# Scoring new tokens four at a time, other slots for their value pages, and adding x at the end in a one-core decoder step

## The chip, the cores and the metric

The kernel runs on one core of a Trainium2 chip. The metric is the device time of one execution in microseconds; the median of the runs is compared. In the text, PE is TensorE (PEld its weight loads), DVE is VectorE, ACT is ScalarE, POOL is GpSimd and SP is SyncE, which issues all DMAs here.

## The reference, cut to what matters

One decoder layer is computed for a prompt of 1024 tokens and for 8 sequences of 4 new tokens each, all in fp32. RMSNorm(x) goes through one input projection. Four heads run a gated linear recurrence (HGRN2), eight heads run forgetting attention (FoX). The gated outputs are concatenated, multiplied by w_out and added to x, and a last RMSNorm follows:

```python
xp = xp + mixer_output(hg_o, hgate, fox_o, fgate, hg_norm_w[l], w_out[l], xp.dtype)
y_prompt = rmsnorm(xp, final_norm_w)
# new tokens: 256 past rows from two cache pages of 128, and the new rows
s = jnp.einsum('bqhd,bkhd->bhqk', q, k) * (D ** -0.5)
s = s + (cq[..., None] - c[:, :, None, :])
p = jax.nn.softmax(where(causal, s, -inf), axis=-1)
o = jnp.einsum('bhqk,bkhd->bqhd', p, v)
```

## The kernel before

The instruction order is written out by hand. Two programs are interleaved on every engine. The **foreground** is the FoX attention of the prompt: 32 steps, one for each head and quarter of the queries (`order`). A step transposes probabilities (T, line 965), weighs the values with them (W, tile `po`), computes scores of later steps (S, tile `ps`), takes exponentials of them (E, line 945 and the division on POOL, line 950) and gates the result (G). The **stream** (`projections`) is all other work: input projections, the new tokens' attention, the output projection.

`PLANS` writes a foreground step as a list of such letters and numbers. A number is a call of `fill`, which pulls pieces from the stream until the sum of their yields, called credits here, reaches the number times a factor. The factors are 7.6, 6.4, 4.4 and 3.0 for the four query quarters, so a step with quarter 0 to 3 draws 7.6, 6.4, 4.4 or 3.0 credits. In the last head pair (steps 24 to 31; quarters 0, 1, 0, 1, 2, 3, 2, 3) they are multiplied by `F3`. A credit is a weight written in the code and no time of the chip. When the foreground has ended, the rest of the stream runs alone.

In the last head pair the stream has this order:

- The end of the last gate projection. Then `wo_open` frees the memory of the normed input, and the remaining output weights are loaded.
- `out_half(tb, c)` for c = 0, 1 and tb = 0 to 3: the first four of eight k blocks of the output projection of prompt block tb, column half c. Each has 12 matmuls of 512 columns and 2.6 credits. x is loaded into a half tile by `x_load`, DVE adds the PSUM result to it (line 1296), and `out_spill` writes it to DRAM scratch `y_s`. With c = 0 it also issues `k_load`, `wo_load`, and at tb = 3 `decode_queries`, which clears a tile on POOL and fills it with eight small ACT copies (line 1132).
- `fox_decode`, the new tokens' attention, in two groups g of four sequences. A group's scores (`Sx[g]`) take for each sequence four key matmuls of 256 columns and four of 32 columns on the new keys (`kd`), 32 query columns wide, so each sequence owns 32 of the 128 PSUM partitions. An fp32 matmul shows as two matmuls in the trace. One sequence is finished before the next begins; it counts 1.9 credits. `soft(g)` is the softmax. The values are two matmuls of 512 columns for each sequence, 0.85 credits each, and one with the new values for each group (`vdf`). Group 0 of the scores stands ahead of `out_half(3, 1)`, group 1 and the values stand behind it.
- `out_proj(0)`, the new tokens' block `out_proj(NB)`, then `out_proj(1)` to `out_proj(7)`. For blocks 0 to 3 the first half is read back from `y_s` into a y tile (`out_load`), k blocks 4 to 7 are accumulated, and DVE adds them (line 1363). Blocks 4 to 7 are done whole.

Key pages use slots 100, 101, 102 and 5, twice. Value pages use slots 28, 4, 0 and 2, twice: the second four are loaded while the first four are used. A load that reuses a slot waits on SP for the readers of the slot, and all later DMAs wait behind it.

Of the kernel before, what the change touches and what calls it, by code (L numbers as in the profile page):

```python
# [70 lines left out]
def tile_hymba(ctx, tc, x_prompt, x_sample, x_b, x_d, cache_k_t, cache_v, cache_logf_t, state_hgrn, page_table,  # L71
# [1035 lines left out]
            SP.dma_start(lr[j * FH:(j + 1) * FH, PAST:], ld_s[j * DT:(j + 1) * DT].rearrange("t h -> h t"))  # L1107

    KT = (100, 101, 102, 5, 100, 101, 102, 5)

    def k_load(j):
        if j < DB:
# [2 lines left out]
                SP.dma_start(kT[:, b], cache_k_t[pages[2 * j + b]].rearrange("o p s -> (o p) s"))  # L1115

    def v_load(j):
        vp = U((28, 4, 0, 2)[j % 4], 1024, a=2)
        for b in range(2):
            SP.dma_start(vp[:, b], cache_v[0, pages[2 * j + b]].rearrange("a s h d -> s (a h d)"))  # L1120

# [14 lines left out]
    def fox_decode():  # L1136
# [35 lines left out]
            V.tensor_copy(PT[g], p[:, :256].rearrange("p (a t) -> p a t", a=2))  # L1172

        for g in range(2):
            if g:
                for j in range(4):
                    v_load(j)
                m_load(4, 0)
                m_load(5, 0)
            Sx.append(ps_pj()[:, :NK])  # L1180
            for j4 in range(4):
                j = 4 * g + j4
                kT = U(KT[j], 1024).rearrange("p (b a s) -> p a b s", b=2, a=4)
                for pr in range(4):
                    q = qb[:, pr, j].rearrange("p h t -> p (h t)")
                    mm(Sx[g][32 * j4:32 * j4 + 32, :PAST], q, kT[:, pr], pr == 0, pr == 3)
                    if pr == 1:
                        yield 0.9
                for pr in range(4):
                    q = qb[:, pr, j].rearrange("p h t -> p (h t)")  # L1190
                    mm(Sx[g][32 * j4:32 * j4 + 32, PAST:], q, kd[:, pr], pr == 0, pr == 3)
                k_load(j + 4)
                yield 1.0
            soft(g)
            yield 0.36
            if g == 0:
                yield None
        SP.dma_start(fw, bcast_row(final_norm_w, D))
        for g in range(2):
            po = ps_pj()  # L1200
            for j4 in range(4):
                j = 4 * g + j4
                vp = U((28, 4, 0, 2)[j4], 1024, a=2)
                for b in range(2):
                    mm(po[32 * j4:32 * j4 + 32], PT[g][:, b, 32 * j4:32 * j4 + 32], vp[:, b], b == 0, False)
                    i = 2 * j4 + b
                    if g == 0 and b:
                        v_load(j + 4)
                    if g and i % 2 == 0 and i < 6:
                        m_split(4 + i // 2, 0)  # L1210
                        if i == 0:
                            m_load(6, 0)
                    yield 0.85
            mm(po, PN[g], vdf, False, True)
            yield 0.85
            od = xd_f[0]
            A.activation(od, po, AF.Copy)
            defer(3, turn_out, g, od)
# [49 lines left out]
    def x_part(tb):  # L1268
        return U(tb // 2 * 2, D, a=2)[:, tb % 2]

    def x_load(tb, c):
        SP.dma_start(x_part(tb), xp[tb * 128:(tb + 1) * 128, 512 * c:512 * c + 512])

    def out_half(tb, c):

# [4 lines left out]
        for k in range(4):  # L1280
            if tb == c == 0:
                if k == 0:
                    m_split(2, 0)
                    m_split(3, 0)
                    wo_split(3, 0)
                if k in (1, 3):
                    for i in (k - 1, k):
                        x_load(i, 0)
            h, l = merged[k, 0]
            mm(ps, h[:, t], woh(k, cs), k == 0, False)  # L1290
            mm(ps, l[:, t], woh(k, cs), False, k == 3)
            mm(ps, h[:, t], wol(k, cs), False, False)
            if k < 3:
                yield 0.65
        yield 0.65
        V.tensor_add(y, y, ps)
        if c == 0:
            if tb < 3:
                wo_split(tb, 1)
            if tb == 2:  # L1300
                wo_split(3, 1)
            for j in ((0,), (1, 3), (2,), ())[tb]:
                k_load(j)
            if tb > 1:
                wo_load(4 + tb)
            if tb == 3:
                decode_queries()
        else:
            for k in (2 * tb, 2 * tb + 1):
                wo_split(4 + k % 4, k // 4)  # L1310
        if c == 0:
            defer(6, x_load, tb, 1)
            defer(4, out_spill, tb, c, y)
        else:
            out_spill(tb, c, y)

    def out_spill(tb, c, y):
        SP.dma_start(y_s[tb][:, 512 * c:512 * c + 512], y)
# [13 lines left out]
    def out_proj(tb, cuts=(0, 512, 1024)):  # L1332
# [4 lines left out]
        for i in range(len(cuts) - 1):  # L1337
            cs = slice(cuts[i], cuts[i + 1])
            ps = ps_pj()[:, :cuts[i + 1] - cuts[i]]
            if tb < NB:  # L1340
                t = slice((tb % 4) * 128, (tb % 4) * 128 + 128)
                k0 = 4 if tb < 4 else 0
                for k in range(k0, KB):
                    h, l = merged[k, tb // 4]
                    mm(ps, h[:, t], woh(k, cs), k == k0, False)
# [51 lines left out]
    def projections():  # L1397
# [26 lines left out]
        for c in range(2):  # L1424
            for tb in range(4):
                yield from out_half(tb, c)
                if c and tb == 2:
                    for us in dec:
                        if us is None:
                            break  # L1430
                        yield us
        yield from dec
        out_load(0)
        m_load(0, 1)
        m_load(1, 1)
        yield from wait_flag("half0")
# [16 lines left out]
            yield from out_proj(tb)  # L1453
        yield from out_proj(7, (0, 512, 768, 1024))

    F3 = 1.8
    stream.append(projections())
    log_forget()
    need("hq0")
# [23 lines left out]
    for n, (pr, i, q) in enumerate(order):  # L1483
# [15 lines left out]
        if pr == 3:  # L1499
            if s == 4:  # L1500
                flags.add("A")
                out_load(NB)
                out_load(1)
    gate_pop(True)
    flags.add("half1")
    while step() is not None:
# [50 lines left out]
```

## Time and profile before

| | us |
|---|---|
| runs (three) | 773.49, 773.97, 775.08 |
| median | 773.97 |
| the profiled execution, its own time | 775.96 |
| its span, first to last instruction | 774.2 |
| PE, PEld, DVE, ACT, POOL busy | 741.8, 665.5, 464.8, 363.5, 315.1 |
| mean granted TensorE clock | 0.985 |

Busy times are sums of the profile. Matmuls are pipelined, so their durations overlap; what a piece of PE work takes is read from start to start.

### The profile page before, as it was taken

How to read it: one execution, taken by the hardware profiler on the slowest of the kernel's cores; microseconds unless marked ns; L12 is line 12 of the kernel's file. 1: busy time of each engine (PE TensorE's matmuls, PEld its weight loads, DVE VectorE, ACT ScalarE, POOL GpSimd, SP SyncE). 2: the span in 40 equal slices, each digit the busy share in tenths (PEclk: the TensorE clock that was granted, in tenths of full speed). 3: DMA queues.
4: the chain of work that ended last, by engine and by line, in shares of the span. 5: the costliest groups of instructions: out<-in, count | busy, mean ns of one | idle time of the engine just before them, and what ended most of it. 6: DMA issues, size and time to landing. Idle time of an engine off the chain costs nothing.

```text
span 774.2 us, 13013 instructions
## 1 busy us (share of the span) xinstructions
PE 741.8 (96%) x4835; PEld 665.5 (86%) x4835; DVE 464.8 (60%) x973; ACT 363.5 (47%) x853; POOL 315.1 (41%) x332
## 2 busy tenths in 40 slices
PE   8999989999999999998999899989999899999996
PEld 7778989998999999998998899979988776577886
DVE  5775554747647565366447844785478776667422
ACT  5663555434242431136546654757466521555322
POOL 0442544364371753726434552536344533232101
PEclk9999999999999999999999999999999999999999
DMA  8211000101221113013001021101111596713521
GB/s 337 93 36 40 1 11 20 60 4 58 82 83 58 55 33 110 28 37 134 28 29 57 29 71 40 57 30 55 55 57 57 188 329 221 260 58 123 199 81 55
DMA packets 27569, 64.99 MB, mean 84 GB/s; under 512 B 5394, under 2 KB 6546, under 8 KB 27506
## 3 DMA queue, kind: packets, MB, share of 16 engines
q1 hardware_dynamic: 27506, 64.16, 24.3%
q8 instruction: 38, 0.62, 0.3%
q14 instruction: 25, 0.20, 0.1%
HBM read 47.27 MB, written 16.88 MB: 83 GB/s over the span
## 4 chain that ended last, share of the span: by engine, by line
PE 73%; DVE 13%; ACT 8%; issue 3%; DMA 2%; POOL 1%; SPq 1%; DVEq 0%; ACTq 0%; POOLq 0%
PE pj L95 53%; PE ps L95 11%; PE po L95 3%; PE pt L965 2%; DVE u L970 2%; DVE u L896 1%; PE pt L95 1%; DVE st L935 1%; ACT u L969 1%; ACT u L945 1%; DMA u<-in_x_prompt_dram 1%; DMA u<-in_w_dram 1%; ACT xhi L269 1%; DVE u L831 1%; DVE u L638 1%
## 5 line engine op out<-in xcount | busy, mean ns | idle before, releaser
L95 PE MATMUL pj<-xhi,u 128*128 128x352 f32 x1152 | 307.2, 331 | 0.9 <-DVE u L487 0.5
L95 PEld LDWEIGHTS pj<-xhi,u 128*128 128x128 f32 x1152 | 206.5, 190 | 3.1 <-DVE u L487 0.8
L95 PE MATMUL pj<-xlo,u 128*128 128x352 f32 x576 | 187.3, 325 | 0.0
L95 PE MATMUL ps<-u,u 128*128 128x64 f32 (+6 forms) x984 | 129.2, 272 | 3.5 <-ACT u L945 2.6
L95 PEld LDWEIGHTS ps<-u,u 128*128 128x128 f32 (+2 forms) x984 | 112.2, 178 | 12.9 <-ACT u L945 4.4
L950 POOL TENSOR_SCALAR u<-u,st 128x128 f32<-128x128 f32 (+3 forms) x64 | 48.7, 762 | 153.4 <-DVE st L948 87.7
L95 PEld LDWEIGHTS pj<-xlo,u 128*128 128x128 f32 x576 | 109.6, 190 | 0.7
L95 PE MATMUL pj<-u,xhi 128*128 128x260 f32 (+1 forms) x384 | 91.7, 332 | 5.7 <-DVE u L526 3.4
L945 ACT ACTIVATE u<-ps,st 128x512 f32<-128x512 f32 (+2 forms) x96 | 55.0, 578 | 50.3 <-DVE st L938 21.4
L95 PEld LDWEIGHTS pj<-u,xhi 128*128 128x128 f32 x384 | 65.2, 195 | 13.9 <-DVE u L526 3.0
L95 PE MATMUL pj<-h,u 128*128 128x512 f32 (+2 forms) x237 | 74.1, 384 | 0.8 <-DVE h L1086 0.8
L699 POOL TENSOR_TENSOR u<-u,u 128x256 f32<-128x256 f32 (+1 forms) x56 | 42.0, 751 | 76.5 <-PE ps L95 76.4
L970 DVE TENSOR_TENSOR u<-pt,u 128x512 fp32r<-128x512 f32 (+1 forms) x80 | 48.5, 632 | 28.4 <-ACT u L969 27.9
L95 PE MATMUL pj<-u,xlo 128*128 128x260 f32 (+1 forms) x192 | 63.8, 333 | 0.0
L969 ACT ACTIVATE u<-pt 128x512 fp32r<-128x512 f32 (+1 forms) x80 | 41.8, 552 | 41.1 <-PE pt L965 33.5
L935 DVE TENSOR_REDUCE st<-ps 128x1 f32<-128x512 f32 (+2 forms) x96 | 53.4, 556 | 12.2 <-PE ps L95 9.6
L95 PE MATMUL po<-u,u 128*128 128x256 f32 (+1 forms) x320 | 52.2, 287 | 8.5 <-DVE u L970 4.5
L95 PEld LDWEIGHTS po<-u,u 128*128 128x128 f32 x320 | 44.3, 189 | 15.4 <-DVE u L970 7.5
L95 PEld LDWEIGHTS pj<-h,u 128*128 128x128 f32 (+1 forms) x237 | 42.4, 186 | 10.3 <-issue 1.5
L95 PE MATMUL pj<-u,u 128*128 128x512 f32 (+3 forms) x174 | 46.1, 434 | 2.4 <-ACT u L1253 1.0
L95 PE MATMUL pj<-w,u 128*128 128x512 f32 (+2 forms) x125 | 47.4, 380 | 0.0
L700 POOL TENSOR_TENSOR u<-u,u 128x256 f32<-128x256 f32 (+1 forms) x56 | 43.6, 778 | 0.0
(252 smaller groups left out, 1147.0 us busy)
## 6 DMA issues: line engine op xcount, KB each, us to landing
u<-in_w_s_dram SPq DMA_DIRECT2D x24, 512.0 KB
out_dram<-u SPq DMA_DIRECT2D x12, 512.0 KB
u<-in_x_b_dram SPq DMA_DIRECT2D x8, 512.0 KB
u<-in_cache_k_t_dram SPq DMA_DIRECT2D x16, 256.0 KB
u<-in_cache_v_dram SPq DMA_DIRECT2D x16, 256.0 KB
m_s<-u SPq DMA_DIRECT2D x7, 512.0 KB
u<-m_s SPq DMA_DIRECT2D x14, 256.0 KB
w<-in_w_out_dram SPq DMA_DIRECT2D x12, 256.0 KB
```

Of the source, the lines that this page charges most:

```text
L95: PE.matmul(out, lhsT, rhs, start=start, stop=stop, skip_group_check=True)
L269: A.activation(xhi[:, k, t0:t0 + n], xt[:, k], AF.Copy)
L638: V.tensor_mul(f, f3[:, :, 0], f3[:, :, 1])
L699: G.tensor_mul(k4[:, :, 0, :], k4[:, :, 0, :], f3[:, eb, 1:2].to_broadcast([128, n, m]))
L700: G.tensor_mul(q4[:, :, 1, :], q4[:, :, 1, :], f3[:, eb, 0:1].to_broadcast([128, n, m]))
L831: V.tensor_copy(hi, vo[:, :, 64 * i:64 * i + 64])
L935: V.tensor_reduce(st[:, m:m + 1], ps, axis=AX.X, op=OP.min)
L945: A.activation(P[:, s], ps, AF.Exp, scale=-1.0, bias=st[:, lo:lo + 1], accum_out=st[:, 2 + m:3 + m])
L950: G.tensor_scalar(P[:, :e], P[:, :e], st[:, 4:5], 1.0, op0=OP.mult, op1=OP.mult)
L965: PE.transpose(p[:, c:c + 128], probs[n, b][:, j * 128:(j + 1) * 128], ident)
L969: A.activation(ph[:, :w], p[:, :w], AF.Copy)
L970: V.tensor_sub(pl[:, :w], p[:, :w], f32(ph[:, :w]))
```

## The change

- **Scores.** The four sequences of a group now take turns: for each of the four head pairs, one key matmul of every sequence, then the small ones in the same way. A group counts 2.46 credits in place of 7.96.
- **Order.** Group 0 of the scores now runs after `out_half(0, 1)`, group 1 after `out_half(2, 1)`; the values still run after `out_half(3, 1)`.
- **Values.** The pages of sequences 0 to 3 go into the key slots 100, 101, 102, 5 as soon as group 1 has read its keys, those of 4 to 7 into 28, 4, 0, 2 ahead of the values. Keys 0, 1 are loaded after `out_half(0, 0)`, keys 2, 3 after `out_half(1, 0)`. The final norm weights (slot 5) are loaded after the values.
- **x.** `out_half` no longer loads x; ACT copies the PSUM result and the spill is issued at once. x is loaded as one row tile for each block and POOL adds it to the read-back half in `out_proj(0)` to `out_proj(3)`.
- **F3** goes from 1.8 to 1.58.

```diff
+    VT = (100, 101, 102, 5, 28, 4, 0, 2)
     def v_load(j):
-        vp = U((28, 4, 0, 2)[j % 4], 1024, a=2)
+        vp = U(VT[j], 1024, a=2)
...
         for g in range(2):
-            if g:
-                for j in range(4):
-                    v_load(j)
-                m_load(4, 0)
-                m_load(5, 0)
             Sx.append(ps_pj()[:, :NK])
-            for j4 in range(4):
-                j = 4 * g + j4
-                kT = U(KT[j], 1024).rearrange("p (b a s) -> p a b s", b=2, a=4)
-                for pr in range(4):
-                    q = qb[:, pr, j].rearrange("p h t -> p (h t)")
-                    mm(Sx[g][32 * j4:32 * j4 + 32, :PAST], q, kT[:, pr], pr == 0, pr == 3)
-                    if pr == 1:
-                        yield 0.9
-                for pr in range(4):
-                    q = qb[:, pr, j].rearrange("p h t -> p (h t)")
-                    mm(Sx[g][32 * j4:32 * j4 + 32, PAST:], q, kd[:, pr], pr == 0, pr == 3)
-                k_load(j + 4)
-                yield 1.0
+            kTs = [U(KT[j], 1024).rearrange("p (b a s) -> p a b s", b=2, a=4) for j in range(4 * g, 4 * g + 4)]
+            qs = [[qb[:, pr, 4 * g + j4].rearrange("p h t -> p (h t)") for j4 in range(4)] for pr in range(4)]
+            for pr in range(4):
+                for j4 in range(4):
+                    mm(Sx[g][32 * j4:32 * j4 + 32, :PAST], qs[pr][j4], kTs[j4][:, pr], pr == 0, pr == 3)
+                if pr == 3:
+                    for j4 in range(4):
+                        v_load(j4) if g else k_load(j4 + 4)
+                yield 0.45
+            for pr in range(4):
+                for j4 in range(4):
+                    mm(Sx[g][32 * j4:32 * j4 + 32, PAST:], qs[pr][j4], kd[:, pr], pr == 0, pr == 3)
+            yield 0.3
             soft(g)
             yield 0.36
-            if g == 0:
-                yield None
-        SP.dma_start(fw, bcast_row(final_norm_w, D))
+            yield None
+        for j in range(4, DB):
+            v_load(j)
+        m_load(4, 0)
+        m_load(5, 0)
...
-                    if g == 0 and b:
-                        v_load(j + 4)
...
+    def x_row(tb):
+        return U((2, 3, 9, 1)[tb], D)
+    def x_load(tb):
+        SP.dma_start(x_row(tb), xp[tb * 128:(tb + 1) * 128])
...
-                if k in (1, 3):
-                    for i in (k - 1, k):
-                        x_load(i, 0)
...
-        V.tensor_add(y, y, ps)
+        A.activation(y, ps, AF.Copy)
...
-            for j in ((0,), (1, 3), (2,), ())[tb]:
+            for j in ((0, 1), (2, 3), (), ())[tb]:
                 k_load(j)
...
-        if c == 0:
-            defer(6, x_load, tb, 1)
-            defer(4, out_spill, tb, c, y)
-        else:
-            out_spill(tb, c, y)
+        out_spill(tb, c, y)
...
                 k0 = 4 if tb < 4 else 0
+                if tb < 4:
+                    G.tensor_add(y[:, cs], y[:, cs], x_row(tb)[:, cs])
...
-                if c and tb == 2:
+                if c and tb in (0, 2):
...
         yield from dec
+        SP.dma_start(fw, bcast_row(final_norm_w, D))
         out_load(0)
+        x_load(0)
...
-    F3 = 1.8
+    F3 = 1.58
...
                 out_load(1)
+                x_load(1)
+                x_load(2)
+            if s == 6:
+                x_load(3)
```

## Rows read from the trace of the kernel before

**Rows 1.** The page, busy time and the chain that ended last, by engine.
```profile
PE 741.8 (96%) x4835; PEld 665.5 (86%) x4835; DVE 464.8 (60%) x973; ACT 363.5 (47%) x853; POOL 315.1 (41%) x332
PE 73%; DVE 13%; ACT 8%; issue 3%; DMA 2%; POOL 1%; SPq 1%; DVEq 0%; ACTq 0%; POOLq 0%
```
**Rows 2.** Windows of the last head pair: stretch, length, busy times, clock, DMA share, GB/s.
```profile
600.00:620.00 20.00, 17.29 (x87) 14.61 (x86) 15.08 (x21) 10.20 (x22) 10.24 (x9) 0.91 0.58 196
620.00:640.00 20.00, 19.54 (x97) 15.10 (x97) 16.02 (x36) 5.99 (x19) 7.41 (x8) 1.00 0.87 313
...
660.00:680.00 20.00, 19.90 (x107) 9.00 (x106) 12.57 (x37) 8.67 (x22) 6.90 (x6) 1.00 0.68 223
...
720.00:740.00 20.00, 20.00 (x89) 16.20 (x88) 8.51 (x15) 5.16 (x17) 1.49 (x1) 1.00 0.45 157
```
**Rows 3.** Timeline of PE, first group of scores: start, duration, engine, line, shapes, count.
```profile
638.13 1.91 PE L95 MATMUL pj<-u,u 128*32 128x256 f32 x8
639.88 0.29 PE L95 MATMUL pj<-kd,u 128*32 128x32 f32 x4
640.01 0.40 PE L95 MATMUL pj<-u,u 128*32 128x256 f32 x1
...
644.75 0.68 PE L95 MATMUL po<-u,u 128*128 128x256 f32 x4
645.36 1.05 PE L95 MATMUL pj<-u,u 128*32 128x256 f32 x4
...
646.59 0.70 PE L95 MATMUL pt<-xd,cc 64*128 64x260 f32 x2
```
**Rows 4.** The same timeline, second group, its first part.
```profile
650.89 1.91 PE L95 MATMUL pj<-u,u 128*32 128x256 f32 x8
...
653.75 0.66 PE L965 MATMUL pt<-cc,u 128*128 128x128 f32 x4
```
**Rows 5.** Chain that ended last, in order of time: rest of the scores, then values.
```profile
654.41 1.23 PE pj L95 x12
...
657.34 0.98 PE pj L95 x4
...
660.07 3.11 PE pj L95 x27
...
663.81 1.86 PE pj L95 x14
...
666.26 0.97 PE pj L95 x2
...
676.93 1.83 PE pj L95 x6
...
680.91 1.05 PE pj L95 x2
```
**Rows 6.** Timeline of PE: values, four sequences in one stretch.
```profile
663.74 1.93 PE L95 MATMUL pj<-u,u 128*32 128x512 f32 x14
665.60 0.66 PE L965 MATMUL pt<-cc,u 128*128 128x128 f32 x4
```
**Rows 7.** Timeline of PE, first output halves; in brackets idle time and releaser.
```profile
611.91 0.49 PE L95 MATMUL pj<-u,u 128*128 128x512 f32 x1 [0.97 <-ACT u L1253]
...
620.57 0.95 PE L95 MATMUL pj<-u,u 128*128 128x512 f32 x3 [0.46 <-DVE u L1296]
```
**Rows 8.** Groups by line and shape: count, busy, mean ns, idle time before.
```profile
L1296 DVE TENSOR_TENSOR u<-u,pj 128x512 f32<-128x512 f32 x8 | 5.5, 684 | 4.8 <-DMA u<-in_x_prompt_dram 4.0 <-PE pj L95 0.8
```
**Rows 9.** The same view, ACT and POOL.
```profile
L969 ACT ACTIVATE u<-pt 128x512 fp32r<-128x512 f32 x22 | 12.6, 595 | 8.7 <-PE pt L965 8.5
L1132 ACT ACTIVATE u<-qd 64x32 f32<-64x32 f32 x8 | 1.8, 228 | 5.1 <-POOL u L1127 5.0
L1365 POOL TENSOR_TENSOR u<-u,u 128x512 f32<-128x512 f32 x1 | 1.3, 1292 | 42.0 <-DVE u L1363 42.0
```
**Rows 10.** Chain in order of time: a 256 KB x load behind eight weight loads.
```profile
613.34 6.39 DMA u<-in_x_prompt_dram
```

More of the change, by code (lines that the diff above doesn't have):

```diff
@@ L1202, in fox_decode @@
                 j = 4 * g + j4
-                vp = U((28, 4, 0, 2)[j4], 1024, a=2)
+                vp = U(VT[j], 1024, a=2)
                 for b in range(2):
@@ L1269, in x_part @@
         return U(tb // 2 * 2, D, a=2)[:, tb % 2]
-    def x_load(tb, c):
-        SP.dma_start(x_part(tb), xp[tb * 128:(tb + 1) * 128, 512 * c:512 * c + 512])
+    def x_row(tb):
+        return U((2, 3, 9, 1)[tb], D)
+    def x_load(tb):
+        SP.dma_start(x_row(tb), xp[tb * 128:(tb + 1) * 128])
     def out_half(tb, c):
```

## The prediction

> **What bounds the kernel now.** I read the page first: PE is busy for 741.8 of 774.2 us and has 73% of the chain that ended last [rows 1]. That alone does not say that PE binds in the stage that changes, so I read windows next. From 620 us PE is busy for 19.54 to 20.00 us of each 20, at the full clock; DVE has at most 16.02, ACT and POOL about half or less, and the DMA share falls from 0.87 to 0.68 [rows 2]. In the tail (720 to 740) PE stays at 20.00 while everything else is idle half the time or more. So in this stage a microsecond of PE work removed is a microsecond of the end, as long as nothing else becomes late. The stretch 600 to 620 is the exception: PE 17.29, mean clock 0.91 [rows 2]. Then I read PE in order of time, to see what the edited pieces take from start to start, since the busy sums count overlapping ends twice.
>
> **Scores: the large term.** One sequence runs from 638.13 to 640.01: 1.88 us, of which the eight key passes take 1.75 (0.22 each, strictly one after another) and the small ones the rest [rows 3]. All eight sequences: 644.75 - 638.13 = 6.62 and 646.59 - 645.36 = 1.23 in the first group [rows 3]; 653.75 - 650.89 = 2.86 [rows 4] and 1.23, 0.98 and 3.11 in the second [rows 5]. Sum 16.03 us, for matmuls that fill 32 of 128 columns of the array.
>
> What do four strips do when their matmuls stand side by side in the queue? The values show it, since they write the same four strips. Fourteen passes of 512 columns, 0.43 us each if a 256-column pass takes 0.22, would take 6.0 one after another; they took 665.60 - 663.74 = 1.86 [rows 6]. The fullest strip has four of them, 4 x 0.43 = 1.72, and 0.14 is the change back to full width. So a strip takes its own sum and the strips run together. The scores of before could not do this, because one sequence had 16 passes in a row: the next sequence starts (640.01) only when the small passes of this one are under way (from 639.88) [rows 3]. In the new order neighbours are always in different strips. A group then takes what one sequence takes, 1.88, plus 0.14, plus some 0.2 to issue 32 small passes where a strip has 8: 2.2 us. Two groups 4.4, and 0.3 for one place where foreground work cuts into the first: 4.7. **Gain 16.0 - 4.7 = 11.3 us.** Bounds: 16.0 - 2 x 1.88 = 12.3 at best; at worst nothing (a rival below).
>
> The Trainium skill speaks against part of this. "TensorE: Matmul & The Clock Gate", Part 3 (Packing small matmuls), says that weight loads overlap running matmuls only when the row group differs, and that matmuls never pass each other; all strips here use all rows. By that the fours would wait for one another, and the gain would be near 0. The 1.86 us above disagree. The same section gives 2.38 times for three column tiles; as an estimate from that page, four at that efficiency (3.2 times) make the gain 11.0.
>
> **Values: a small loss.** Their PE work is unchanged, but what one piece costs depends on its neighbours. Of 18 pieces (sixteen page matmuls, two `vdf`), before, seven stood together (1.86), three together (1.83), and eight stood in seven short runs of 0.97 to 1.05 between full-width work, first and last shown [rows 5]: 10.7 us. I place the new order by credits. At F3 = 1.58 the steps 24 to 28 draw 12.0, 10.1, 12.0, 10.1 and 7.0, in sum 51.2. The stream has about 7.7 of the gate projection, five `out_half` (13.0), group 0 (2.5; at 20.7 to 23.1, the end of step 25 and the start of 26), two `out_half`, group 1 (28.3 to 30.8, inside one fill of step 26), `out_half(3, 1)`, and the values from 33.4 to 48.7. In steps 26 to 28 that makes one long run of about nine pieces (4.6: two strips' worth on either side of a `vdf`) and about eight short ones of 1.0. **Loss 12.7 - 10.7 = 2.0 us**; bounds 0, if they fall as before, and 18 x 0.97 - 10.7 = 6.8, if all stand alone; I take 2.0 because the credits give the runs.
>
> **x out of `out_half`.** DVE loses eight adds of 0.684, 5.5 us, and a 4.0 us wait for the first x load [rows 8], a 256 KB load that took 6.39 us behind eight weight loads [rows 10]. But of that wait PE felt only 0.46 [rows 7]. ACT gains eight PSUM copies, nearest row 0.595 [rows 9], 4.8 us on an engine that is half idle; it waits there for matmuls that PE reaches anyway. **Gain 0.5 us.** The three PE waits from 611.9 on, 0.8 to 1.0 each, first one shown [rows 7], wait for splits of m and w_out, which stay; so the stretch of that window at the lower clock level, which cost 0.09 x 20 = 1.8 us, stays too. It can go, or come twice: bounds -2 to +2.
>
> POOL gains eight 128x512 adds, 1.29 each [rows 9], 10.3 us. Four lie in the tail, where POOL has 1.5 of 20. The DVE add of a half now waits for the POOL add, which waits for two loads; both are issued a whole block ahead, save for block 0.
>
> **New waits.** (a) `decode_queries`' eight ACT copies, 8 x 0.228, stand behind the copy of `out_half(3, 0)`, 0.6: ready 2.4 us after that half, and only `out_half(0, 1)`, 12 x 0.225 = 2.7 [rows 2], covers them: 0 to 1. (b) Values 0 to 3 are issued at credit 30.1. Until the first is used PE has the rest of group 1, `out_half(3, 1)` and one foreground score, 4.8 us; until the eighth load is used some 10. The queue moves 313 GB/s at a share of 0.87 [rows 2], so 0.73 us for 256 KB at full share, 5.8 for eight; and 2 MB of x loads have left it. Behind a full queue a load took 6.39 [rows 10], so the first may cost up to 1.6. (c) Values 4 to 7 and m 4, 5 queue on SP behind a spill, and are wanted about 8 us after: 0 to 1. (d) Rows y and x for block 0 (1 MB) are issued when the last value has run; POOL's add waits for them, and with it the later softmax divisions, needed two steps on. The DVE add stands behind about 8 us of PE work; 2 x 512 KB take 2.9 us at full share plus about 3 to start, then 1.3 for the add, 7.2: hidden by about 1 us, with a bound of 2. In sum 0 to 5.6; the cover holds in each, so I take 0.8.
>
> **F3.** It removes no work. Steps 24 to 31 draw 42.8 x 1.58 = 67.6 credits in place of 77.0, while the stream up to the same place lost 11.0, so the foreground ends a little further along in `out_proj(1)` and the same PE-bound tail follows: 0, with a price only if a foreground step waits for its own chain (below).
>
> **Sum.** -11.3 + 2.0 - 0.5 + 0.8 = -9.0 us. The profiled execution took 775.96, 1.8 beyond its span, and would take 767.0. It lies 2.0 above the median of the runs, 773.97, so I forecast 773.97 - 9.0 = **765.0 us**.
>
> **Rivals.**
> - *All of it arrives*: the values fall as before and no wait shows: -11.3 - 0.5 = -11.8, 762.2 us. For it: PE's full windows. Against it: shorter fills cut the values oftener. 0.14.
> - *Late data or a thin filler eats half*: waits (b) to (d) come near their bounds, or steps 26 to 28, with less filler, wait for ACT and DVE: 4.5 more, 769.5 us. For it: DVE at 16.02 of 20 from 620 [rows 2]. Against it: DVE loses 5.5 us, and the same foreground steps had a factor of 1.0 in the earlier heads. 0.17.
> - *The fours run one after another*, so the change does not do what it says: the scores stay at 16.0, and the values' cuts, +2.0, and 0.8 of waits less 0.5 remain: +2.3, 776.3 us, slower. It decides if a strip must empty before the next may load weights, which the page above would have; then order is no matter. Against it: the 14 passes in 1.86 us. 0.05.
> - *The end is not PE's*: some other chain holds the foreground's end, and the gain turns into PE idle time: about 773, no change. Against it: PE 20.00 of 20 through the tail. 0.03.
>
> **How the numbers follow.** The forecast has 0.61, with its own range 763 to 767.5. The range 761.5 to 769.5 takes in the first two rivals' centres and leaves out about 0.2. About 0.2%, 1.5 us, can be told from no change. Slower: 0.05 from the serial case, less the part of it that would stay within the bound, 0.04. Same: the rest of that, and the fourth rival, 0.04. Faster 0.92.
>
> **What would show it.** A group of scores of 2.0 to 2.5 us on PE, its 32 key passes inside 2 us; about 8 us would be the serial case. The values at 12 to 13 us. No DVE wait for x near 617, the PE wait of 0.46 gone, those for the splits still there. PE windows at 19.5 or more of 20 from 625 to the end. Idle PE time in front of the first value, of W, or of `out_proj(0)`'s second half would be the late-data rival. The forecast is wrong if the scores shrink as said and PE shows over 3 us of new idle time.

## The result: 0.9% slower, and the profile after

The changed kernel took 781.15 us (780.34 to 781.51) beside 773.97: ratio 1.0092 [1.0072, 1.0112]. The forecast was 765.0 us. Its profiled execution took 781.51 us, span 779.7, mean clock 0.981; the one of before 775.96, 774.2 and 0.985.

The page's busy line, beside [rows 1]:

```profile
PE 738.8 (95%) x4835; PEld 662.6 (85%) x4835; DVE 465.7 (60%) x965; ACT 368.1 (47%) x861; POOL 328.8 (42%) x340
```

The windows that answer to [rows 2], with three more: stretch, length, busy times, clock, DMA share, GB/s.

```profile
620.00:640.00 20.00, 19.97 (x146) 15.26 (x144) 13.94 (x34) 8.90 (x25) 8.38 (x8) 1.00 0.83 292
640.00:660.00 20.00, 18.93 (x130) 9.56 (x129) 13.57 (x39) 6.82 (x19) 6.27 (x7) 1.00 0.81 279
660.00:680.00 20.00, 19.90 (x92) 10.99 (x91) 9.16 (x24) 8.82 (x19) 7.87 (x8) 1.00 0.42 144
680.00:700.00 20.00, 18.07 (x100) 13.64 (x99) 13.74 (x32) 11.90 (x32) 6.75 (x7) 1.00 0.37 131
700.00:720.00 20.00, 16.07 (x70) 12.96 (x69) 13.21 (x18) 7.29 (x18) 9.40 (x6) 0.83 0.34 103
720.00:740.00 20.00, 17.77 (x77) 13.87 (x76) 10.45 (x14) 6.60 (x18) 6.68 (x5) 1.00 0.51 180
```

Up to 680 us PE is nearly as full as before. From 680 to 740 it is busy for 51.9 of 60 us, where before had 59.7 (20.00, 19.68 and 20.00), and in 700 to 720 the mean clock is 0.83. The loss sits in the last steps of the foreground and the first output blocks, behind the scores and the values, where the additions of x now run.

The pieces themselves, on PE's timeline (start, duration, engine, line, shapes, count, idle time and releaser), beside [rows 3 to 6]:

```profile
629.89 1.50 PE L95 MATMUL pj<-u,u 128*32 128x256 f32 x24
632.31 0.64 PE L95 MATMUL pj<-u,u 128*32 128x256 f32 x8
632.77 0.56 PE L95 MATMUL pj<-kd,u 128*32 128x32 f32 x32
...
641.06 0.59 PE L95 MATMUL pj<-u,u 128*32 128x256 f32 x2 [0.37 <-DMA u<-in_cache_k_t_dram]
642.35 0.59 PE L95 MATMUL pj<-u,u 128*32 128x256 f32 x2 [0.70 <-DMA u<-in_cache_k_t_dram]
...
644.67 0.56 PE L95 MATMUL pj<-kd,u 128*32 128x32 f32 x32
...
656.19 1.05 PE L95 MATMUL pj<-u,u 128*32 128x512 f32 x4
...
657.65 1.91 PE L95 MATMUL pj<-u,u 128*32 128x512 f32 x6
659.50 1.12 PE L95 MATMUL pj<-vdf,u 32*128 32x512 f32 x2
660.55 1.90 PE L95 MATMUL pj<-u,u 128*32 128x512 f32 x6
...
662.97 1.05 PE L95 MATMUL pj<-u,u 128*32 128x512 f32 x2
...
672.26 1.12 PE L95 MATMUL pj<-vdf,u 32*128 32x512 f32 x2
```

The first group of scores takes 1.43 and 0.94 us in its two parts, 2.37 in sum, where 2.2 was forecast; the second takes 5.09 from start to end, because keys 4 to 7 come late (waits of 0.37 and 0.70 us) and 0.48 us of softmax transposes of the new tokens are cut in. Without the transposes, the scores take 7.0 us in sum in place of 16.0. The values fall into eight single matmuls, one run of two and two runs of three, besides the two `vdf`: 14.6 us in place of 10.7.

And the waits that PE has afterwards, with the DVE and POOL instructions at the same time:

```profile
682.66 0.62 PE L95 MATMUL po<-u,u 128*128 128x256 f32 x3 [0.99 <-DVE u L970]
...
692.60 0.63 PE L95 MATMUL po<-u,u 128*128 128x256 f32 x3 [0.94 <-DVE u L970]
...
706.70 1.01 PE L95 MATMUL po<-u,u 128*128 128x256 f32 x3 [3.09 <-DVE u L970]
...
721.51 0.50 PE L95 MATMUL pj<-h,u 128*128 128x512 f32 x1 [0.79 <-DVE u L1358]
...
728.70 2.33 PE L95 MATMUL pj<-u,u 128*128 128x512 f32 x9 [1.44 <-DVE u L1358]
```

```profile
690.48 1.46 DVE L1378 SCALAR_TENSOR_TENSOR u<-u,so,u 128x512 f32<-128x512 f32 x2 [0.60 <-ACT so L219]
...
702.72 3.32 DVE L1378 SCALAR_TENSOR_TENSOR u<-u,so,u 32x512 f32<-32x512 f32 x2 [0.59 <-ACT so L219]
705.97 1.27 DVE L970 TENSOR_TENSOR u<-pt,u 128x512 fp32r<-128x512 f32 x2
...
718.11 2.75 DVE L1378 SCALAR_TENSOR_TENSOR u<-u,so,u 128x512 f32<-128x512 f32 x2 [0.60 <-ACT so L219]
```

```profile
702.56 2.93 POOL L1337 TENSOR_TENSOR u<-u,u 128x512 f32<-128x512 f32 x2
...
716.86 3.45 POOL L1337 TENSOR_TENSOR u<-u,u 128x512 f32<-128x512 f32 x2
```

L1378 is the last scaling of an output block, with two inputs in SBUF; L1337 is the new addition of x on POOL, also with two. Away from the additions, a pair of scalings takes 1.46 us. Beside a pair of additions it takes 2.72 to 3.32, and the additions get longer too. Behind the stretched pair in DVE's queue stands L970, the subtraction that W needs, and PE waits 3.09 us for it. All 128-row scalings have a mean of 940 ns here; before it was 778. The Trainium skill, "SBUF — State Buffer", section "SBUF: two separate sides", says that VectorE and GpSimd take one pair of ports in turns, for a whole instruction each, when the VectorE instruction has two SBUF inputs. This trace agrees in the main: the four instructions together are over in 3.48 us, nearer to the sum of both pairs alone (1.46 + 2.6) than to the longer one, but 0.6 us short of that sum.

**An account of PE's tail.** For each profile I take the time from the last matmul of the gate projection to the end. I add up PE's idle times in brackets in it (waits), and (1 - granted clock) times length over windows of 5 us up to PE's last matmul (clock). The rest is PE work with its starts. F3 and the ratio stand beside it. The columns for scores and values are times from start to start. Each kernel has one profile, of an execution within 2.0 us of the median of its runs, save for e3 and i1 (2.6 and 2.8 below), g2 and g3 (5.1 and 3.2 below) and g4 (3.9 above): tails of these can't be compared closer than that.

| kernel | F3 | tail | waits | clock | rest | scores, values | ratio |
|---|---|---|---|---|---|---|---|
| before | 1.8 | 165.0 | 3.5 | 1.7 | 159.8 | 16.0, 10.7 | 1 |
| after | 1.58 | 171.1 | 11.4 | 5.1 | 154.6 | 7.0, 14.6 | 1.0092 |
| e1_f3 | 1.8 | 166.6 | 10.1 | 5.2 | 151.3 | 6.8, 11.1 | 1.0007 |
| e2_noadd | 1.58 | 163.6 | 6.4 | 1.7 | 155.5 | 7.2, 14.6 | 0.9972 |
| e3_dve | 1.58 | 168.8 | 11.3 | 1.7 | 155.8 | 7.0, 14.6 | 1.0086 |
| e4_xback | 1.58 | 173.6 | 10.1 | 8.5 | 155.0 | 12.7, 14.6 | 1.0076 |
| f1_noadd_f3 | 1.8 | 160.9 | 7.1 | 1.7 | 152.1 | 6.4, 11.7 | 0.9965 |
| f2_fours | 1.8 | 166.9 | 10.7 | 5.1 | 151.1 | 11.0, 10.4 | 1.0034 |
| f3_f158 | 1.58 | 170.8 | 4.7 | 3.4 | 162.7 | 16.0, 12.8 | 1.0057 |
| f4_early | 1.7 | 163.5 | 8.7 | 3.4 | 151.4 | 7.4, 11.5 | 0.9965 |
| g1_keys | 1.58 | 171.2 | 11.0 | 6.8 | 153.4 | 4.7, 14.6 | 1.0063 |
| g2_mix17 | 1.7 | 164.5 | 10.9 | 3.4 | 150.2 | 4.5, 11.5 | 1.0016 |
| g3_mix18 | 1.8 | 166.0 | 11.7 | 3.4 | 150.9 | 4.5, 11.2 | 1.0024 |
| g4_mix158 | 1.58 | 170.0 | 10.1 | 6.8 | 153.1 | 4.7, 14.6 | 1.0023 |
| h1_early158 | 1.58 | 168.4 | 9.2 | 5.2 | 154.0 | 6.6, 14.6 | 1.0042 |
| h2_keys17 | 1.7 | 162.0 | 8.7 | 3.4 | 149.9 | 4.7, 11.5 | 0.9957 |
| h3_early18 | 1.8 | 166.6 | 10.0 | 5.1 | 151.5 | 6.5, 11.1 | 1.0015 |
| i1_xback_keys17 | 1.7 | 161.6 | 8.7 | 3.4 | 149.5 | 6.3, 11.5 | 0.9956 |
| i2_noadd1 | 1.58 | 169.1 | 9.3 | 5.1 | 154.7 | 6.0, 14.6 | 1.0051 |
| i3_noadd_keys17 | 1.7 | 160.0 | 6.8 | 3.4 | 149.8 | 5.6, 11.5 | 0.9928 |

So the change did take work from PE: 5.2 us by this account (159.8 to 154.6). It gave back 7.9 us in waits and 3.4 us at the lower clock. The clock term also counts time in which PE stood idle, so it overlaps the waits: weighted by PE's busy share of each window it is 3.9 us in after and 1.5 in before, which would make the work removed 4.2 us and the clock's part 2.4.

### The profile page after: what moved, and what is told of

Read it like the earlier page. It is cut to its first block, busy times and chain, and to the rows that moved or that the text cites. A ratio compares the mean times of both kernels' runs of the same rounds, so it can differ in the third digit from the quotient of the medians.

```text
span 779.7 us, 13013 instructions
## 1 busy us (share of the span) xinstructions
PE 738.8 (95%) x4835; PEld 662.6 (85%) x4835; DVE 465.7 (60%) x965; ACT 368.1 (47%) x861; POOL 328.8 (42%) x340
## 5 line engine op out<-in xcount | busy, mean ns | idle before, releaser
L95 PE MATMUL po<-u,u 128*128 128x256 f32 (+1 forms) x320 | 54.2, 292 | 14.0 <-DVE u L970 9.2
L970 DVE TENSOR_TENSOR u<-pt,u 128x512 fp32r<-128x512 f32 (+1 forms) x80 | 48.3, 631 | 28.9 <-ACT u L969 28.2
L95 PEld LDWEIGHTS po<-u,u 128*128 128x128 f32 x320 | 45.4, 192 | 23.0 <-DVE u L970 12.8
L935 DVE TENSOR_REDUCE st<-ps 128x1 f32<-128x512 f32 (+2 forms) x96 | 53.4, 556 | 11.2 <-PE ps L95 8.5
L95 PEld LDWEIGHTS pj<-h,u 128*128 128x128 f32 (+1 forms) x237 | 43.4, 190 | 11.3 <-issue 1.2
L95 PE MATMUL pj<-u,u 128*128 128x512 f32 (+3 forms) x174 | 39.7, 434 | 4.4 <-DVE u L1358 1.4
```

The source lines that it names most:

```text
L95: PE.matmul(out, lhsT, rhs, start=start, stop=stop, skip_group_check=True)
L935: V.tensor_reduce(st[:, m:m + 1], ps, axis=AX.X, op=OP.min)
L970: V.tensor_sub(pl[:, :w], p[:, :w], f32(ph[:, :w]))
```

## The experiments

Ratios are to the kernel before, on the same chip, with their 95% interval. e2, f1 and i3 leave x out of the first four prompt blocks, i2 out of the second.

### One part undone at a time

**e1_f3**, F3 back.

```diff
-    F3 = 1.58
+    F3 = 1.8
```

> The changed kernel with F3 back at 1.8, nothing else. Theory A (collision): what was lost is PE waiting for DVE, because POOL's adds of x run beside DVE instructions with two SBUF inputs and stretch them (the final scaling took 3.32 us for two in place of about 1.5). Then a larger F3 mends little: 778 to 783 us. Theory B (thin filler): the last foreground steps have too little other work between a transpose and the weighing that needs it, because of F3 = 1.58. Then most of the 11 us of PE idle time and lower clock go: 769 to 773 us.

Measured 1.0007 [0.999, 1.0024], between the two expectations and 6.6 us better than after. The values are at 11.1 us, but the collision is there, only elsewhere:

```profile
708.99 3.01 DVE L1378 SCALAR_TENSOR_TENSOR u<-u,so,u 128x512 f32<-128x512 f32 x2 [0.60 <-ACT so L219]
```

```profile
712.65 0.62 PE L95 MATMUL po<-u,u 128*128 128x256 f32 x3 [2.52 <-DVE u L970]
```

**e2_noadd**, no additions and loads of x.

```diff
-                if tb < 4:
-                    G.tensor_add(y[:, cs], y[:, cs], x_row(tb)[:, cs])
...
-        x_load(0)
...
-                x_load(1)
-                x_load(2)
-            if s == 6:
-                x_load(3)
```

> The changed kernel without the eight POOL adds and the four loads of x that feed them; x is left out of the first four prompt blocks. Theory A (collision): the stretched DVE instructions and the PE waits behind them go, 768 to 772 us. Theory B (thin filler): the waits for the copies of transposed probabilities stay, 778 to 781 us.

Measured 0.9972 [0.9954, 0.9989], 9.3 us better than after, as theory A has it. The 3.09 us wait is 1.18, the waits for L1358 are down to 0.17 in sum, the clock from 700 to 740 is 1.00, and the scalings are back at 773 ns. Of the 5.0 us by which PE's waits shrink, 4.0 stood behind stretched scalings (1.91 at the 3.09 us wait, 0.79 and 1.27 for L1358), and 0.8 at block 0, where nothing is stretched: there DVE's addition of the half waits for POOL's, and L970 stands behind it (after, then e2):

```profile
682.66 0.62 PE L95 MATMUL po<-u,u 128*128 128x256 f32 x3 [0.99 <-DVE u L970]
```

```profile
681.83 0.62 PE L95 MATMUL po<-u,u 128*128 128x256 f32 x3 [0.19 <-DVE u L970]
```

The additions, with the loads that feed them, are the largest single part of the loss, though POOL is busy less than half the time. This run takes out both; i2 below takes out additions alone.

**e3_dve**, the same additions on DVE.

```diff
-                    G.tensor_add(y[:, cs], y[:, cs], x_row(tb)[:, cs])
+                    V.tensor_add(y[:, cs], y[:, cs], x_row(tb)[:, cs])
```

> The changed kernel with the eight adds of x on DVE in place of POOL, same loads, same place. Theory A (collision): no POOL work of that size beside DVE, but eight more DVE instructions of 0.7 us, four of them while the foreground still runs: 770 to 775 us. Theory B (thin filler): DVE is later still, 780 to 785 us.

Measured 1.0086 [1.0063, 1.0109], in theory B's range, but not for its reason. The scalings are at 754 ns, so the collision needs POOL; but now DVE's queue stops at block 0's addition until its row of x has landed, and PE's next transposes wait behind it; the profile puts that down to the instruction in front of them on DVE:

```profile
679.28 0.66 PE L965 MATMUL pt<-cc,u 128*128 128x128 f32 x4 [2.67 <-DVE mo L1226]
```

This run trades one cost for another and does not price the collision.

**e4_xback**, x loaded and added in `out_half` as before.

```diff
+                if k in (1, 3):
+                    for i in (k - 1, k):
+                        x_load(i, 0)
...
-        A.activation(y, ps, AF.Copy)
+        V.tensor_add(y, y, ps)
...
-        out_spill(tb, c, y)
+        if c == 0:
+            defer(6, x_load, tb, 1)
+            defer(4, out_spill, tb, c, y)
+        else:
+            out_spill(tb, c, y)
```

> The changed kernel with the x part undone: x loaded into the half tiles and added by DVE in out_half, deferred spill, no row tiles, no POOL adds; scores, value slots, order and F3 as changed. Theory A (collision): 769 to 773 us, since the score gain stays and the collision goes. Theory B (thin filler): 778 to 782 us.

Measured 1.0076 [1.0046, 1.0105], in theory B's range, again for another reason. The x loads now stand before keys 4 to 7 on SP's queue, and the second group waits three times, 3.9 us in sum, the longest here; in 650 to 655 the granted clock is 0.51.

```profile
646.41 0.59 PE L95 MATMUL pj<-u,u 128*32 128x256 f32 x2 [2.58 <-DMA u<-in_cache_k_t_dram]
```

So with the fours at this place, taking x out of `out_half` is worth more than the 0.5 us that I gave it: it clears the queue ahead of the keys. With keys asked for earlier (i1 against h2, below) it is worth nothing that can be measured.

### Parts alone, and combined

**f1_noadd_f3**: e2 with F3 = 1.8.

```diff
-    F3 = 1.58
+    F3 = 1.8
```

> The changed kernel without the POOL adds and their x loads (x is left out of the first four prompt blocks), and F3 at 1.8. Either edit alone gave 6 and 9 us back. If they take away two separate causes (stretched DVE instructions, and too little other work in the last steps): 766 to 769 us. If both only ease the same waits for transposed probabilities: 771 to 774 us.

Measured 0.9965 [0.9938, 0.9992]. F3 is worth 0.85% with the additions (e1 against after) and nothing that can be measured without them (f1 against e2). The two costs are not two terms to be added.

**f2_fours**: before, with the fours at the old places.

```diff
-            for j4 in range(4):
-                j = 4 * g + j4
...
-                k_load(j + 4)
-                yield 1.0
+            for pr in range(4):
+                for j4 in range(4):
+                    mm(Sx[g][32 * j4:32 * j4 + 32, :PAST], qs[pr][j4], kTs[j4][:, pr], pr == 0, pr == 3)
...
+                        k_load(4 * g + j4 + 4)
```

> The kernel before with the scores in fours alone, at their old places, x and value slots and F3 as before. If score time is PE time that reaches the end: 11 us less, 764 to 766 us. If the pages then come too late, because keys 4 to 7 are asked for only when all four of the first group are read and values 0 to 3 only when group 1 begins: PE waits for keys and values of some 3 to 4 us each, 769 to 773 us.

Measured 1.0034 [1.0013, 1.0056], slower than both expectations. Group 0 shows the fours undisturbed. Group 1 then waits 4.3 us in sum for its keys, for these were issued one sequence at a time before and now only behind the whole of group 0:

```profile
636.56 1.93 PE L95 MATMUL pj<-u,u 128*32 128x256 f32 x32
...
644.03 0.59 PE L95 MATMUL pj<-u,u 128*32 128x256 f32 x2 [1.55 <-DMA u<-in_cache_k_t_dram]
...
647.66 1.03 PE L95 MATMUL pj<-u,u 128*32 128x256 f32 x2 [1.49 <-DMA u<-in_cache_k_t_dram]
```

Besides, after 670 us PE waits 3.8 us for ACT and DVE, where before waits 0.3, with neither an addition on POOL nor a lower F3.

**f3_f158**: before, with F3 alone.

```diff
-    F3 = 1.8
+    F3 = 1.58
```

> The kernel before with F3 = 1.58 alone. If the smaller share is harmless while PE is full, as forecast: 773.5 to 775.5 us. If it leaves the last foreground steps waiting for their own chain (transpose, ACT copy, DVE subtraction, weighing): 778 to 782 us.

Measured 1.0057 [1.0035, 1.0079], as the second expectation has it. The values rise from 10.7 to 12.8 us, the rest from 159.8 to 162.7. In each of the pairs that differ in F3 alone (e1 and after, f1 and e2, h3 and h1, before and f3, g3 and g4) the lower F3 has 2.2 to 3.4 us more rest, and the values alone take 2.1 to 3.5 us more. Besides, a chain is uncovered early:

```profile
620.87 0.63 PE L95 MATMUL po<-u,u 128*128 128x256 f32 x3 [1.77 <-DVE u L970]
```

**f4_early**: additions one block earlier, F3 = 1.7.

```diff
-                if tb < 4:
-                    G.tensor_add(y[:, cs], y[:, cs], x_row(tb)[:, cs])
...
+        x_add(0)
         yield from out_proj(0)
         yield from wait_flag("A")
+        x_add(1)
         yield from out_proj(NB)
         for tb in (1, 2, 3):
+            if tb == 2:
+                yield from wait_flag("x3")
+            if tb < 3:
+                x_add(tb + 1)
...
-    F3 = 1.58
+    F3 = 1.7
```

> The changed kernel with each pair of POOL adds one block earlier, away from the final scaling on DVE, and F3 = 1.7. If the collision of these two and the thin filler are the causes: 768 to 772 us, faster than before. If POOL's adds cost DVE time wherever they stand: 775 to 779 us.

Measured 0.9965 [0.9948, 0.9983], faster than before, as the first expectation has it. Why, only the next two tell.

**h1_early158** and **h3_early18**: f4 with the other values of F3.

```diff
-    F3 = 1.7
+    F3 = 1.58
```

> After, with GpSimd's x additions one block earlier and F3 left at 1.58: of the two losses only the collision of additions and final scalings is taken away. Theory C (the collision makes the slower result by itself; F3 is worth little once it is gone): 0.995 to 0.999 of before (771 to 774 us), scaling pairs at 1.5 us, no wait above 2 us for L970 or L1358 after 700 us. Theory F (the smaller filler bound makes it by itself, as F3=1.58 alone cost the kernel before 4.4 us): 1.004 to 1.008 (778 to 781 us), values 14.6 us and W passes over 16 us in the account of PE's tail. If both are needed together for the loss (either cover is enough), it reads as theory C with values still at 14.6 us.

```diff
-    F3 = 1.7
+    F3 = 1.8
```

> Early x additions with F3=1.8 as before the change, so only the edits on scores, values and x remain. Theory of a reserve of other work (F3 1.58 only cuts the values and W's into shorter pieces): values 11 to 12 us, ratio 0.994 to 0.998 (770.5 to 773.5 us), not better than F3=1.7 by more than 1 us. Rival (each step of F3 back towards 1.8 gives about 2 us): 0.990 to 0.993.

Measured 1.0042 [1.0025, 1.0059] and 1.0015 [1.0, 1.0029]: h1 comes out as theory F has it, values and W included (18.2 us from start to start, of which 6.0 are waits); but h3, with more filler still, misses both of its expectations on the slow side. So the size of F3 is not the mechanism either, and the lines tell what is. In h1 the early additions meet another scaling, again ahead of L970 (POOL, DVE, PE):

```profile
688.89 2.98 POOL L1278 TENSOR_TENSOR u<-u,u 128x512 f32<-128x512 f32 x2
```

```profile
689.92 2.50 DVE L1382 SCALAR_TENSOR_TENSOR u<-u,so,u 128x512 f32<-128x512 f32 x2 [0.60 <-ACT so L219]
```

```profile
693.07 0.63 PE L95 MATMUL po<-u,u 128*128 128x256 f32 x3 [1.97 <-DVE u L970]
```

In h3 they meet the next one, with L970 still behind it:

```profile
710.67 3.16 DVE L1382 SCALAR_TENSOR_TENSOR u<-u,so,u 128x512 f32<-128x512 f32 x2 [0.60 <-ACT so L219]
```

```profile
714.49 0.63 PE L95 MATMUL po<-u,u 128*128 128x256 f32 x3 [2.65 <-DVE u L970]
```

In f4 the stretched pair is as long, but it starts behind the last L970 of the foreground, and costs PE 1.16 us at a block's addition:

```profile
709.87 3.23 DVE L1382 SCALAR_TENSOR_TENSOR u<-u,so,u 128x512 f32<-128x512 f32 x2 [0.60 <-ACT so L219]
```

```profile
714.60 0.50 PE L95 MATMUL pj<-h,u 128*128 128x512 f32 x1 [1.16 <-DVE u L1362]
```

So by these profiles F3, besides the cuts in the values, sets which stretched pair stands before the foreground's chain. Of the three values tried, 1.7 is the one at which none does; that says nothing of F3 in itself.

**i2_noadd1**: after, without block 1's two additions, the pair at 702.56.

```diff
-                if tb < 4:
+                if tb in (0, 2, 3):
```

> After, with only block 1's two GpSimd additions left out (x is missing from that block's output). They run at 702.6 us beside the scaling pair of the new tokens' block, which took 3.32 us there and held L970, for which PE waited 3.09 us, and the clock fell behind that. Theory A (that one collision makes most of the loss): the pair at 1.4 to 1.7 us, no wait above 1.5 us for L970 after 700, ratio 1.001 to 1.005 (775 to 778.5 us). Rival (PE waits there for something else that is late by as much): 1.007 to 1.011.

Measured 1.0051 [1.003, 1.0072], at the upper end of theory A; the interval just reaches the rival. Against after, whose interval it just touches, one pair of additions cost 3.2 us by the centres; the loads stay in this run.

```profile
702.52 1.40 DVE L1378 SCALAR_TENSOR_TENSOR u<-u,so,u 32x512 f32<-32x512 f32 x2 [0.59 <-ACT so L219]
```

```profile
704.58 0.92 PE L95 MATMUL po<-u,u 128*128 128x256 f32 x3 [1.18 <-DVE u L970]
```

The pair and the wait are as theory A has them: this collision made 1.9 of the 3.09 us. The other half of the foreseen gain would have come from the clock, but the mean of 700 to 720 is 0.91 here, not 1.00.

### Earlier keys

**g1_keys**: after, group 0 and the query copies earlier.

```diff
-            if tb == 3:
+            if tb == 1:
                 decode_queries()
...
-                if c and tb in (0, 2):
+                if (c, tb) in ((0, 3), (1, 2)):
```

> The changed kernel with group 0 of the scores ahead of all second halves (after out_half(3, 0)) and decode_queries after out_half(1, 0), nothing else. Keys 4 to 7 then have three output halves to arrive in place of two. If late keys hold PE: the two waits of 0.4 and 0.7 us and the breaks around them go, scores from 7.0 to about 5 us, time about 2 us below the changed kernel, 778 to 781 us. If the loss lies only further on: 781 to 783 us.

Measured 1.0063 [1.0034, 1.0092], by the centres 2.2 us better than after as foreseen, but with intervals that overlap. No wait for keys is left and the scores take 4.7 us, what I had forecast for the change itself:

```profile
641.00 2.07 PE L95 MATMUL pj<-u,u 128*32 128x256 f32 x32
```

The collisions stay as in after, 3.09 us included.

**g2_mix17**, **g3_mix18**, **g4_mix158**: g1 with early additions, block 3's on DVE, at three values of F3.

```diff
-            G.tensor_add(y[:, cs], y[:, cs], x_row(tb)[:, cs])
...
+            (V if tb == 3 else G).tensor_add(y[:, cs], y[:, cs], x_row(tb)[:, cs])
```

> The changed kernel with early group 0 as in the first run of this set, POOL adds of x for blocks 0 to 2 one block earlier, those of block 3 on DVE, and F3 = 1.7. If collision, late keys and thin filler are the whole loss: 766 to 770 us. If something else holds the end: 771 to 774 us.

> The same mix with F3 = 1.8. If a thin filler still costs at 1.7: 1 to 2 us faster than that run. If only the place of the POOL adds matters: the same within 1 us.

> The same mix with F3 = 1.58. If the thin filler costs by itself, as in the kernel before (4 us there): 3 to 4 us slower than with 1.8. If it costs only where stretched DVE work adds to it: within 1 us.

Measured 1.0016 [1.0003, 1.003], 1.0024 [1.0007, 1.0041] and 1.0023 [1.0006, 1.004]. The scores are at 4.5 to 4.7 us in all, but g2 has a new wait of 3.64 us: the query copies, now two halves earlier on ACT, wait there for POOL to clear their tile, and a copy of the foreground waits behind them. g2 misses both of its expectations on the slow side, and its profile is the fastest of its runs, so it doesn't show what holds the median. g3 and g4, at 1.8 and 1.58, can't be told apart in time, though the values take 11.2 and 14.6 us: the lower F3 costs by itself in before, and nothing that can be measured in this mix.

**h2_keys17**: f4 with group 0 as in g1, the query copies only one half earlier.

```diff
-            if tb == 3:
+            if tb == 2:
                 decode_queries()
```

> The version with early x additions and F3=1.7, with score group 0 one output half-block earlier (after out_half(3,0)) so that keys 4 to 7 land before group 1, and the query copies only one half-block earlier than in after, not two, so that ScalarE isn't held by the 0.95 us memset on GpSimd behind which the copies waited at 618 to 621 us in the run with two. Theory K (the late keys cost PE's own path, 2.4 us): scores 4.5 to 4.9 us, ratio 0.993 to 0.995 (769 to 771 us). Rival (in these steps PE has slack that another wait takes up, as in the run of after with earlier keys): scores 4.5 to 4.9 us, but ratio 0.996 to 0.999, with a wait on L969, L970 or L1358 longer by as much.

Measured 0.9957 [0.9942, 0.9973], between the two expectations and not to be told from f4. The keys' gain comes (scores 4.7 us in place of f4's 7.4), and a wait for the same copies takes most of it back:

```profile
630.60 2.15 PE L95 MATMUL pj<-u,u 128*32 128x256 f32 x31 [2.10 <-POOL u L1128]
```

**i1_xback_keys17**: h2's keys, queries and F3, x as in e4.

```diff
-                    G.tensor_add(y[:, cs], y[:, cs], x_row(tb)[:, cs])
...
+        V.tensor_add(y, y, ps)
...
+    F3 = 1.7
```

> The fours with early keys (group 0 after out_half(3,0), queries after out_half(2,0)) and F3=1.7, but x loaded and added by VectorE in out_half as before the change: no GpSimd addition of x anywhere. Theory A (the GpSimd additions are what costs in the steps after 685 us): no wait for L970 above 1.2 us there, no wait for the block adds in the tail, ratio 0.985 to 0.992 (763 to 768.5 us). Rival (the x loads in front of keys 4 to 7 are the larger cost, 3.9 us of waits and a lower clock when they were put back alone): waits for keys of 2 us or more and 0.996 to 1.003.

Measured 0.9956 [0.9938, 0.9973], between the two expectations: no wait for L970 above 0.34 after 685 us and none above 0.23 in the tail, as theory A has it, and no long wait for keys either, but 2.66 us for the cleared query tile and 1.09 for a value page. h2, with x added by POOL, has the same time: at these places the choice of engine for x is worth nothing that can be measured.

**i3_noadd_keys17**: the same without x.

```diff
-                if tb < 4:
-                    G.tensor_add(y[:, cs], y[:, cs], x_row(tb)[:, cs])
...
-            if tb == 3:
+            if tb == 2:
                 decode_queries()
...
-                if c and tb in (0, 2):
+                if (c, tb) in ((0, 3), (1, 2)):
...
+    F3 = 1.7
```

> Early keys, F3=1.7, and neither the loads nor the additions of x (x is missing from the first four blocks' output): beside the same version with early additions (771.26 us, 0.9957) it gives what is left of their cost. Theory A: 0.988 to 0.993 (765.5 to 769.5 us), the waits of 1.08 and 1.13 us for the block adds gone. Rival (at F3=1.7 the additions already cost nothing): 0.994 to 0.997.

Measured 0.9928 [0.9909, 0.9946], in theory A's range, with an interval that reaches the rival's. By the centres x still costs some 0.3% at the best place found (h2 against this, with intervals that overlap), and even without x this order of work is 5 us under before, not 9.

Three versions that compute all beat both kernels: f4, h2 and i1, by 2.6 to 3.5 us under the before of their own batch.

## Why the prediction was wrong, point by point

- **Scores, -11.3.** The mechanism was right: 32 key passes take 1.93 (f2) to 2.07 us (g1), against what "TensorE: Matmul & The Clock Gate", Part 3 (Packing small matmuls), of the Trainium skill says of weight loads and row groups. The term measured -9.0 in after and -11.3 in g1. What failed is a wait that the list of new waits does not hold: `k_load(4)` to `k_load(7)` moved behind the last key of group 0, and I followed the value loads past that point, not the keys.
- **Values, +2.0.** Measured +3.9. The credits gave the eight single matmuls. The run of nine came too, but cut by softmax transposes and its `vdf` into 2, 3, 1 and 3: 5.7 us (656.19 to 662.38 less 0.47 of transposes) in place of 4.6. And nine and eight are 17 of the 18 pieces: the sum leaves out the second `vdf`, 1.06 us.
- **F3: 0.** "It removes no work" looks at the sum of credits. A smaller number means shorter fills: 2.2 to 3.4 us more of PE work in five pairs, and a different place for everything behind. F3 alone made before slower by 0.57%; in two of the pairs (f1 and e2, g3 and g4) the times can't be told apart.
- **x, -0.5, and "POOL gains eight 128x512 adds ... Four lie in the tail, where POOL has 1.5 of 20".** This is the step that failed most: 0 was the price, and 9.3 us came between after and e2, in waits behind stretched scalings, a plain wait at block 0 and the lower clock. I asked whether POOL had time, not what its reads do to DVE's. The trace of before held the sign, and I took one duration from it: of another POOL instruction of the same size (L1254) the mean is 1524 ns where the one in [rows 9] has 1292, and pairs of the scaling spread from 1.42 to 1.67 us.
- **New waits, (a) to (d), +0.8.** Of (b) and (c) nothing shows in after. (d) came: POOL's addition for block 0 began 5.1 us after the first of its two loads was issued (673.41 to 678.53; the sum had 5.9), it held DVE for 0.71 us, and PE's wait there is 0.99 in place of e2's 0.19. (a) is covered in after; a wait for the same copies came in h2, i1 and i3, at 2.1 to 2.7 us, but for POOL's clearing of their tile, which the sum does not hold.
- **"A microsecond of PE work removed is a microsecond of the end, as long as nothing else becomes late."** The condition failed. i3 has 10.0 us less rest than before, yet its tail is only 5.0 shorter: 3.3 more are waits, 2.1 of them for the query tile, and 1.7 the lower clock. With less PE work beside them, the foreground's copies and subtractions are no longer covered: after 670 us PE waits for ACT and DVE 0.3 us in before, 2.0 in i3 and 3.8 in f2.
- **Rivals.** *Late data or a thin filler* named the right chain, ACT and DVE behind steps with less filler, but priced its waits at 4.5 us and gave the clock nothing. Waits and clock came to 11.3 (10.3 without the overlap), more than the work removed, which is why the sign turned.

What stays open: the additions cost 0.4% with F3 at 1.8 (e1 and f1) and 1.2% at 1.58 (after and e2). Whether the lower clock in after follows from the waits behind the stretched pairs is not shown, since the clock did not answer alike to like waits (below).

## What to carry to other kernels

A free engine is not a free operation: before moving an elementwise operation to GpSimd, look whether VectorE has instructions with two SBUF inputs at that place, and what stands behind them in its queue. A weight that only sets how pieces are dealt out is a change of the whole order behind it, so it must be set again after each edit, and what it gives there is no property of the edit. Where an edit gathers several loads' last readers into one place, follow each load to its next use.

## What the runs showed of the hardware

- A pair of 32-row scalings took 3.32 us beside two 128-row additions on POOL and 1.40 without them (after, i2); 128-row pairs beside such additions took 2.50 to 3.23 (after, e1, f4, h1, h3), so fewer rows did not lose less.
- L970, which reads one input from PSUM, took 0.68 us at 692.34 in h1 while POOL was in a two-input instruction (L1014, 691.83 to 693.55); L1361, with two SBUF inputs, went from 0.68 to 1.73 beside an addition in the same profile.
- After the 3.09 us wait of after, the granted clock was 0.54 in 705 to 710, mostly the lower of its two levels (1.2 of 2.4 GHz), and 0.78 in 710 to 715, with PE at 2.77 of 5 us in 700 to 705. Passes of 512 columns then started 0.43 us apart (707.50 and 707.93), and 0.23 apart from 712.32. Waits of 0.65 and 1.18 us at the same place left the clock at 1.00 in e2, and in i2 it fell to 0.69 in 705 to 710. Which of the two follows is not to be read from the waits alone. The windows of after, i2 and e2:

```profile
705.00:710.00 5.00, 3.31 (x12) 2.91 (x13) 2.24 (x3) 0.34 (x1) 0.50 (x1) 0.54 0.54 179
```

```profile
705.00:710.00 5.00, 5.00 (x24) 4.35 (x23) 1.36 (x3) 0.49 (x1) 0.00 (x0) 0.69 0.54 187
```

```profile
700.00:720.00 20.00, 18.01 (x88) 14.59 (x87) 14.15 (x23) 10.06 (x26) 6.24 (x4) 1.00 0.39 131
```
